# Seven block products for the convolution and gate columns of a fused two-block kernel

## The chip, the cores and the metric

One core of a Trainium2 chip runs the whole program, two residual blocks on a sequence of 1024 tokens of width 1024, in float32 accuracy. The metric is the device time of one execution in microseconds (us), lower is better.

## The reference, cut to what matters

The first block (an HGRN2 mixer and an MLP) is not touched by the change. The second block is

```python
def hybrid_mixer(u, w_in, conv_w, conv_norm_g, ret_norm_g, w_out):
    z = u @ w_in                                    # 1024 x 3584
    cb, cc, ch = jnp.split(z[..., :c0], 3, axis=-1) # 512 columns each
    rq, rk, rv, rg = jnp.split(z[..., c0:], 4, axis=-1)
    y_conv = cb * causal_dwconv3(cc * ch, conv_w)
    y_conv = group_rms_norm(y_conv, conv_norm_g, CONV_GROUPS)   # 8 groups of 64
    q, k = rotary(rq), rotary(rk) * 128 ** -0.5     # 4 heads of 128
    o = chunkwise_retention(q, k, rv)
    y_ret = group_rms_norm(o, ret_norm_g, RET_HEADS) * jax.nn.silu(rg)
    return jnp.concatenate([y_conv, y_ret], axis=-1) @ w_out

h = x + hybrid_mixer(rms_norm(x, norm1_g), ...)
h = h + sq_relu_mlp(rms_norm(h, norm2_g), w_up, w_down)
```

## The kernel before, in words

Activations lie transposed: a tile holds 128 channels (partitions) of all 1024 tokens, in two halves of 512. Every product of float32 is three matmuls in the fp32r type (`mm3`, L200 to L205): each operand is split into a high part (`hi`, `uh`; a cast on ACT) and the rest (`lo`, `ul`; a subtraction on DVE, or on POOL where `self.low` says so), and hi x hi, hi x lo and lo x hi are summed in PSUM. A weight slab is 128 x 1024 (512 KB): it is loaded, split (`split_next`) and used as the stationary operand by `unit`, which makes one output tile for one half of the tokens from eight k tiles, 24 matmuls of 512 columns.

The program is written out once, and the order of the lines is the order on each engine: the engines take their own instructions strictly in turn. Work for the other engines is put between the matmuls by `self.at(delay, fn)`, which has `fn` issued at the end of the tick that comes `delay` ticks later; a `tick` is called after every 12 matmuls of 512 columns. The tables of numbers at the head of the file (`RETENTION_AT` and the like) are such delays. `use` splits a slab now and those up to `look` further on one tick later, and issues the loads; all DMAs are issued by one queue, SP. `slots` is a ring of tiles of 4 KB a partition in SBUF, `bank` and `accb` give PSUM banks, four of each kind.

The MLPs already multiply by seven block products: `expand` makes, for a pair of weight tiles or of operand tiles, the four blocks and the four sums and differences f and g (L832 to L838 for weights, L856 to L862 for operands), splits them, and `group` runs the products in the order P1, P2, P3, P5, P6, P7, P4. `project` multiplies by `w_out`, adds the residual and prepares the MLP's operands.

`mixer2` (L1399 to L1542) goes through these stages. **Values** (about 1192 to 1245 us): the columns of rv, with the token tiles `u` as stationary operand and 256 columns of the weights moving, the first four token chunks k tile by k tile (L1454), the others one after another; the row norms come from PE's `stats` and `turn`, and the residual is rescaled in place (L1444). **Heads** (to 1356): for each of four heads a q and a k slab, rotation on ACT and DVE (L1483 to L1487) and `retention`, whose steps follow by `RETENTION_AT`; its head norm runs in twelve small operations on POOL (L249 to L256) 13 ticks later, and the head's output stays in SBUF as `on[h]`. **Columns** (to 1504): for each of four tiles the slabs cc, ch, cb, with the convolution on ACT and DVE and, per half, `conv_norm`: squares, two matmuls with a matrix of two blocks of ones (L1559), and an iteration for the root on DVE. **Gates** (to 1549): four slabs, Silu and product with `on`. `split_y` (L1496, L1497) splits the convolution's output into the operands of **project** (from 1549), with the low halves on POOL.

Of the kernel before, what the change touches and what calls it, by code (L numbers as in the profile page):

```python
# [11 lines left out]
F32 = mybir.dt.float32  # L12
# [8 lines left out]
P = 128  # L21
# [17 lines left out]
CONV_NORM_AT = (2, 4, 5)  # L39
CONV_SPLIT_AT = (55, 56, 59, 59)  # L40
# [19 lines left out]
HIDDEN_BY = "GVVV"  # L60

# [9 lines left out]
C_CW, C_CG, C_RG, C_ZETA, C_BLK = 320, 332, 336, 340, 344  # L71
C_N = 346
# [25 lines left out]
class Kernel:  # L98
# [483 lines left out]
    def gate(self, ps, half, on, yh, yl, done=None):  # L582
        nc = self.nc
        tk = slice(half * HALF, (half + 1) * HALF)
        z = self.times_rb(ps, half)
# [12 lines left out]
        self.at(GATE_AT[0], product)  # L598
        self.at(GATE_AT[1], low)
# [12 lines left out]
    def run(self):  # L612
# [50 lines left out]
        self.ac = S.get("ac")  # L663
# [45 lines left out]
        self.blocks = sm.tile([P, P], F32R, name="blocks")  # L709

        def set_masks():
            copy = nc.scalar.copy
            for i in range(2):
# [7 lines left out]
            copy(self.blocks.rearrange("p (g f) -> p g f", g=2),  # L721
                 self.col(C_BLK, 2)[:, :, None].to_broadcast([P, 2, 64]))
# [3 lines left out]
        for a in (*self.a_bufs, self.ac[:, :512]):  # L726
            nc.gpsimd.memset(a, 0.0)
# [51 lines left out]
        S.put(*self.a_bufs, self.ac, self.rb)  # L779
# [3 lines left out]
        sp, us, rb = self.project(y, None, C_NMLP, True)  # L783
# [147 lines left out]
    def project(self, y, x, gain, first):  # L931
# [467 lines left out]
    def mixer2(self, x, u, sqs):  # L1399
        nc, S = self.nc, self.slots  # L1400
        self.rb = rb = S.get("rb")
        rx = S.get("rx")
        cos, sin, dx = S.get("cos"), S.get("sin"), S.get("dx")
# [39 lines left out]
        def normed(j):  # L1443
            nc.vector.scalar_tensor_tensor(x[j], x[j], self.col(C_NFIN + j), rx, op0=MUL, op1=MUL)  # L1444
# [55 lines left out]
        for i in range(4):  # L1500
            if i == 0:
                for n in range(4):
                    self.at(CONV_SPLIT_AT[n], lambda n=n: split_y(n))
            cc, yc = S.get("cc"), S.get("yc")
            for part in range(3):
                ws = self.use()
                for half in range(2):
                    tk = slice(half * HALF, (half + 1) * HALF)
                    ps = self.unit(ws[0], u, half)
                    if part == 0:  # L1510
                        nc.vector.tensor_tensor(cc[:, tk], ps, rb[:, tk], op=MUL)
                    elif part == 1:
                        z = self.times_rb(ps, half)
                        nc.vector.tensor_tensor(cc[:, tk], cc[:, tk], z, op=MUL)
                        if half == 1:
                            w = lambda j: self.col(C_CW + 4 * j + i)
                            nc.scalar.activation(yc, cc, AF.Copy, scale=w(2))
                            nc.vector.scalar_tensor_tensor(yc[:, 1:], cc[:, :-1], w(1), yc[:, 1:], op0=MUL, op1=ADD)
                            nc.vector.scalar_tensor_tensor(yc[:, 2:], cc[:, :-2], w(0), yc[:, 2:], op0=MUL, op1=ADD)
                            S.put(cc)  # L1520
                    else:
                        z = self.times_rb(ps, half)
                        nc.vector.tensor_tensor(yc[:, tk], yc[:, tk], z, op=MUL)
                        self.conv_norm(i, yc, half, y)
                self.done(ws)

        self.low = nc.gpsimd
        for j in range(4):
            ws = self.use()
            for half in range(2):  # L1530
                ps = self.unit(ws[0], u, half)
                if half == 0:
                    y[4 + j] = (S.get("yh", F32R), S.get("yl", F32R))
                self.gate(ps, half, lambda j=j: on[j], *y[4 + j],
                          done=(lambda j=j: S.put(on[j])) if half else None)
            self.done(ws)
        self.drain()
        S.put(rb)
        for a in u:
            S.put(*a)  # L1540
        self.low = nc.vector
        return self.project(y, x, C_N2, False)  # L1542

    def conv_norm(self, i, yc, half, y):

        nc, S = self.nc, self.slots
        tk = slice(half * HALF, (half + 1) * HALF)
        A, B = slice(0, HALF), slice(HALF, T)
        n1, n2, n3 = S.get("n1"), S.get("n2", F32R), S.get("n3")
        sq, ms, hi, lo, z, t = n1[:, A], n1[:, B], n2[:, A], n2[:, B], n3[:, A], n3[:, B]  # L1550
        dv = nc.vector
        nc.scalar.activation(sq, yc[:, tk], AF.Square)
        nc.scalar.copy(hi, sq)
        nc.gpsimd.tensor_tensor(lo, sq, hi.bitcast(F32), op=SUB)

        def stat():
            ps = self.bank()
            nc.tensor.matmul(ps, lhsT=self.blocks, rhs=hi, start=True, stop=False)
            nc.tensor.matmul(ps, lhsT=self.blocks, rhs=lo, start=False, stop=True)  # L1559
            dv.tensor_scalar(ms, ps, 1.0 / 64, EPS, op0=MUL, op1=ADD)  # L1560
            dv.tensor_scalar(z.bitcast(I32), ms.bitcast(I32), -0.5, 1597463007.0, op0=MUL, op1=ADD)
# [170 lines left out]
```

## Time and profile before

| | us |
|---|---|
| median of 3 runs | 2269.64 (2268.79 to 2270.84) |
| the profiled execution | 2272.97 |
| its span in the profile | 2270.8 |
| PE busy | 2239.4 (99%) |
| DVE busy | 1768.2 (78%) |
| ACT busy | 880.3 (39%) |
| POOL busy | 405.1 (18%) |

The profile comes from one execution; its own time is 2.2 us more than its span. A row of the timeline gives when an instruction began, how long it lasted, its line, and in brackets how long the engine was idle before it and what ended that. Matmuls overlap each other, so what one costs is read from start to start. In rows of PE the text behind the arrow is the moving operand, then the stationary one.

### The profile page before, as it was taken

What the parts mean: (1) busy time and instruction counts of PE and PEld (TensorE: products, weight loads), DVE (VectorE), ACT (ScalarE), POOL (GpSimd) and SP (SyncE); (2) the same over time, 40 slices, a digit from 0 to 9 for tenths busy, and PEclk for the clock granted to TensorE, in tenths of its full rate; (3) what the DMA queues carried; (4) which work ended last, traced back from release to release, by engine and by line L of the source; (5) the groups of instructions that cost most, each with busy time, mean ns of one, the idle gap of its engine ahead of it and who ended that gap; (6) DMA issues with size and microseconds to landing.
All of it is one profiled execution on the core that took longest, in us unless ns stands there. A gap on an engine that the chain in (4) does not pass through costs nothing.

```text
span 2270.8 us, 32900 instructions
## 1 busy us (share of the span) xinstructions
PE 2239.4 (99%) x13102; PEld 1884.9 (83%) x13102; DVE 1768.2 (78%) x2593; ACT 880.3 (39%) x1346; POOL 405.1 (18%) x381
## 2 busy tenths in 40 slices
PE   8999999999999999999999999999999999999998
PEld 7888797888888888888889888887888888888887
DVE  6857668636888888999996556885698888889996
ACT  6334433434433335434344242224533334533322
POOL 0122112201111111222210011013111111122223
PEclk9999999999999999999999999999999999999999
DMA  4011010123344448444512011112234446744442
GB/s 179 25 36 39 20 38 29 47 76 128 120 169 161 151 168 299 158 148 154 194 43 103 28 40 35 47 38 75 94 137 164 158 153 210 260 152 148 158 158 75
DMA packets 80218, 261.91 MB, mean 115 GB/s; under 512 B 8896, under 2 KB 11456, under 8 KB 80064
## 3 DMA queue, kind: packets, MB, share of 16 engines
q1 hardware_dynamic: 79488, 259.28, 32.8%
q8 instruction: 103, 1.69, 0.3%
q10 hardware_dynamic: 576, 0.52, 0.1%
q14 instruction: 51, 0.42, 0.1%
HBM read 186.37 MB, written 73.40 MB: 114 GB/s over the span
## 4 chain that ended last, share of the span: by engine, by line
PE 86%; DVE 10%; ACT 2%; issue 1%; DMA 1%; SPq 0%; DVEq 0%; ACTq 0%
PE acc L203 20%; PE acc L204 20%; PE acc L205 20%; PE ps L203 7%; PE ps L205 7%; PE ps L204 7%; PE ps L543 1%; PE ps L545 1%; PE ps L523 1%; DVE tmp L579 1%; PE ps L305 1%; DVE tmp L590 1%; DVE ac L389 1%; PE ps L454 0%; DVE lo L174 0%
## 5 line engine op out<-in xcount | busy, mean ns | idle before, releaser
L203 PE MATMUL acc<-hi,hi 128*128 128x512 f32 (+1 forms) x824 | 315.1, 382 | 0.7 <-ACT acc L1226 0.6
L204 PE MATMUL acc<-lo,hi 128*128 128x512 f32 (+1 forms) x824 | 313.9, 381 | 0.7 <-POOL lo L1497 0.7
L205 PE MATMUL acc<-hi,lo 128*128 128x512 f32 (+1 forms) x824 | 313.8, 381 | 0.0
L203 PE MATMUL acc<-uh,hi 128*128 128x512 f32 x768 | 306.6, 399 | 0.0
L204 PE MATMUL acc<-ul,hi 128*128 128x512 f32 x768 | 300.2, 391 | 0.0
L205 PE MATMUL acc<-uh,lo 128*128 128x512 f32 x768 | 300.2, 391 | 0.0
L203 PE MATMUL ps<-hi,hi 128*128 128x512 f32 x712 | 277.2, 389 | 0.0
L205 PE MATMUL ps<-hi,lo 128*128 128x512 f32 x712 | 277.0, 389 | 0.0
L204 PE MATMUL ps<-lo,hi 128*128 128x512 f32 x712 | 277.0, 389 | 0.0
L1169 ACT ACTIVATE hq<-hq 128x512 f32<-128x512 f32 x128 | 81.1, 634 | 336.9 <-DVE hq L1168 269.9
L203 PEld LDWEIGHTS acc<-hi,hi 128*128 128x128 f32 x824 | 154.9, 188 | 31.8 <-ACT acc L1226 1.5
L204 PEld LDWEIGHTS acc<-lo,hi 128*128 128x128 f32 x824 | 154.9, 188 | 31.1 <-POOL lo L1497 1.2
L205 PEld LDWEIGHTS acc<-hi,lo 128*128 128x128 f32 x824 | 154.9, 188 | 29.5
L205 PEld LDWEIGHTS acc<-uh,lo 128*128 128x128 f32 x768 | 144.7, 188 | 31.0
L203 PEld LDWEIGHTS acc<-uh,hi 128*128 128x128 f32 x768 | 144.9, 189 | 30.4 <-ACT v L608 0.2
L204 PEld LDWEIGHTS acc<-ul,hi 128*128 128x128 f32 x768 | 144.9, 189 | 28.9 <-issue 0.5
L204 PEld LDWEIGHTS ps<-lo,hi 128*128 128x128 f32 x712 | 133.6, 188 | 27.9
L205 PEld LDWEIGHTS ps<-hi,lo 128*128 128x128 f32 x712 | 133.6, 188 | 27.7
L203 PEld LDWEIGHTS ps<-hi,hi 128*128 128x128 f32 x712 | 133.6, 188 | 27.7
L180 ACT CAST hi<-h 128x1024 fp32r<-128x1024 f32 x96 | 100.4, 1055 | 134.0 <-DVE lo L181 76.6
L181 DVE TENSOR_TENSOR lo<-h,hi 128x1024 fp32r<-128x1024 f32 x96 | 122.2, 1280 | 6.3 <-ACT hi L180 6.3
L174 DVE TENSOR_TENSOR lo<-w,hi 128x1024 fp32r<-128x1024 f32 x70 | 84.9, 1220 | 49.5 <-ACT hi L173 49.5
(271 smaller groups left out, 4720.5 us busy)
## 6 DMA issues: line engine op xcount, KB each, us to landing
w<-in_w SPq DMA_DIRECT2D x202, 512.0 KB, 4.5
hf<-f SPq DMA_DIRECT2D x28, 512.0 KB, 2.6
hfull<-hq SPq DMA_DIRECT2D x28, 512.0 KB, 3.5
hg<-g SPq DMA_DIRECT2D x28, 512.0 KB, 4.0
h<-hfull SPq DMA_DIRECT2D x28, 512.0 KB, 3.6
h<-hf SPq DMA_DIRECT2D x28, 512.0 KB, 4.4
h<-hg SPq DMA_DIRECT2D x28, 512.0 KB, 3.3
xs<-x SPq DMA_DIRECT2D x16, 512.0 KB, 2.8
```

What stands on the lines that cost most here:

```text
L174: self.low.tensor_tensor(lo, st, hi.bitcast(F32), op=SUB)
L180: self.nc.scalar.copy(hi, src)
L181: self.low.tensor_tensor(lo, src, hi.bitcast(F32), op=SUB)
L203: mm(ps, lhsT=ah, rhs=bh, start=start, stop=False)
L204: mm(ps, lhsT=ah, rhs=bl, start=False, stop=False)
L205: mm(ps, lhsT=al, rhs=bh, start=False, stop=stop)
L305: self.nc.tensor.matmul(ps[:, :n * P], lhsT=self.cs[:, C_ONES:C_ONES + P], rhs=b[:, :n * P], start=True, stop=True)
L389: ve.copy_predicated(av[:, j:], mask[:, v0:v1], pm[:, v0:v1])
L523: nc.tensor.matmul(ps[:, c * P:(c + 1) * P], lhsT=kt[:, t], rhs=v[:, t], start=True, stop=True)
L543: nc.tensor.matmul(o, lhsT=a3[:, i, :], rhs=v[:, t], start=True, stop=(i == 0))
L545: nc.tensor.matmul(o, lhsT=qx[:, t], rhs=s[:, t], start=False, stop=True)
L1169: nc.scalar.activation(t, t, AF.Square)
```

## The change

The 16 slabs of cc, ch, cb and the gates become 8 pairs. For a pair, two output tiles of all 1024 tokens come from seven products instead of eight (each over four pairs of k tiles, 12 matmuls of 512 columns), with blocks of the weights expanded as in the MLP, all sums on POOL (`CONV_BY`), and blocks of the operand: B11, B21, B22 are halves of `u`, the others are sums f and g of the tiles. These sums are made from the scaled residual during the values stage (`block_sums`: two copies of 1024 on ACT, two adds on POOL and two on DVE for each of four pairs of tiles), stored to DRAM, loaded again in the last head and split; f goes over a half of `u`. `four` combines the products into the four quarters of output and hands each to the stage's `out` as PSUM tile and summand. A first and a second pair make cc x ch of two tiles, the third their cb.

The values take 512 columns of weights at a time, four slabs used one after another with `look` 1. `conv_norm` takes two tiles together: eight matmuls with selection matrices bring all sums of squares into one bank, the root is iterated once, and eight matmuls spread it. The residual and the heads' outputs go through DRAM. The matrix `sel` is loaded from a fourth table. In `project` the first tile's second half comes first. The order of the slabs in DRAM follows. A line number of the changed file is 8 higher than before in the helpers (L174 becomes L182, L832 L840, L1497 is now L1640).

```diff
-CONV_NORM_AT = (2, 4, 5)
-CONV_SPLIT_AT = (55, 56, 59, 59)
+BLOCKS_AT = (1, 3, 5, 6)
+T2_AT = (2, 2, 3, 3)
+G_AT = (1, 1, 2, 2)
+CONV_W0_AT = (0, 1, 2, 2, 2, 3)
+CONV_W_AT = (3, 4, 5, 5, 5, 6)
+NORM_AT = (0, 4, 5, 6, 7, 9)
+CONV_SPLIT_AT = (1, 2, 12, 13)
+LATE_SPLIT_AT = (3, 4)
+BLOCKS_BY = "GVGV"
+CONV_BY = "GGGG"
...
 def project(self, y, x, gain, first):
-                if x is None:
-                    xs[j] = S.get("x")
-                    nc.sync.dma_start(xs[j], self.x_dram[j])
-                else:
-                    xs[j] = x[j]
+                xs[j] = S.get("x")
+                nc.sync.dma_start(xs[j], x[j])
                 ws = self.use()
-                for half in range(2):
+                for half in ((1, 0) if n == 0 and not first else (0, 1)):
...
 def mixer2(self, x, u, sqs):
         def normed(j):
...
+            nc.sync.dma_start(xn_dram[j], x[j])
+            S.put(x[j])
...
+        def block_sums(kp):
+            st = {"1": S.get("us"), "2": S.get("us")}
+            for n, j in (("1", kp), ("2", kp + 4)):
+                nc.scalar.activation(st[n], x[j], AF.Copy, scale=self.gg[:, j:j + 1])
+            e = self.expand(st, "B", self.by(BLOCKS_BY))
+            e["sums_f"]()
+            e["sums_g"]()
...
+        for kp in range(4):
+            self.at(BLOCKS_AT[kp], lambda kp=kp: block_sums(kp))
+        self.look = 1
...
+        for n, k in enumerate(order):
+            if n % 2 == 0:
+                ws[k] = self.use()[0]
             for t in range(4):
-                self.col_b(ws, u, t, (k,), banks[t][:, :256], (order[0], order[-1]))
+                values_k(t, k, banks[t])
+            self.tick()
...
+                if h == 3 and dst is k:
+                    w_next = self.prep_w(pairs, CONV_W0_AT, CONV_BY)
+                    for kp in range(4):
+                        self.at(kp, lambda kp=kp: load_blocks(kp, "f"))
+                        self.at(T2_AT[kp], lambda kp=kp: split_t2(kp))
...
+        for kp in range(4):
+            split_t1(kp)
+            self.at(G_AT[kp], lambda kp=kp: load_blocks(kp, "g"))
+            self.at(G_AT[kp] + 2, lambda kp=kp: split_g(kp))
...
+        def pair(out, last=False):
+            i = n_pair[0] = n_pair[0] + 1
+            w = w_next
+            if i < 8:
+                w_next = self.prep_w(pairs + 2 * i, CONV_W_AT, CONV_BY)
+            self.load_to(pairs + 2 * i + 2)
...
+            self.group(w, us, 0, self.four(out), free)
...
+        for i in (0, 2):
+            pair(product(i))
+            pair(product(i + 1))
...
+            pair(gated(i))
+        self.low = p
+        for n in range(4):
+            self.at(CONV_SPLIT_AT[n], lambda n=n: split_y(n))
+        pair(gates(0))
+        self.next_split = self.next_use = pairs + 16
+        self.limit = SECOND_MLP
+        self.at(6, self.split_next)
+        for n in range(2):
+            self.at(LATE_SPLIT_AT[n], lambda n=n: split_y(4 + n))
+        pair(gates(2), True)
...
+        return self.project(y, xn_dram, C_N2, False)
+    def four(self, emit):
...
+        def out(name, ps):
+            if name == "P1":
+                st["p1"] = self.tmp()
+                nc.scalar.copy(st["p1"], ps)
+            elif name in ("P2", "P3", "P5"):
+                st[name] = ps
+                if name == "P2":
+                    emit(0, 0, ps, st["p1"])
+            elif name == "P6":
+                u2 = st["u2"] = self.tmp()
+                v.tensor_tensor(u2, ps, st["p1"], op=ADD)
+                t = self.tmp()
+                v.tensor_tensor(t, st["P5"], u2, op=ADD)
+                emit(0, 1, st["P3"], t)
+            elif name == "P7":
+                u3 = st["u3"] = self.tmp()
+                v.tensor_tensor(u3, ps, st["u2"], op=ADD)
+                emit(1, 1, st["P5"], u3)
+            else:
+                emit(1, 0, ps, st["u3"])
...
 def conv_norm
+        def total(n):
...
+            for c in (A, B):
+                nc.tensor.matmul(st["ps"], lhsT=of(n, 0), rhs=t[:, c], start=(n, c) == (0, A), stop=(n, c) == (3, B))
...
+        def fin(n):
...
+            for c in (A, B):
+                nc.tensor.matmul(ps, lhsT=of(n, 1), rhs=st["s"][:, c], start=c == A, stop=c == B)
+            o = yc[i + r][:, (A, B)[h]]
+            v.scalar_tensor_tensor(o, ps, self.col(C_CG + i + r), o, op0=MUL, op1=MUL)
...
 def retention
+            nc.sync.dma_start(to, on)
```

Three places show how the order moved. The first is DVE at the start of the values stage. `lo` is the low half of a weight slab, `sqs` and `sqg` are sums of squares, `f` and `g` block sums of x, `us` its scaled copy. Before:

```order
L281 SCALAR_TENSOR_TENSOR ul_920_11128<-x_586_8470,gg_6013,uh_919_11127 128x512
L271 TENSOR_TENSOR sqs_897_10777<-sqs_897_10777,tmp887_11156 128x512
L271 TENSOR_TENSOR sqg_898_10778<-sqg_898_10778,tmp888_11158 128x512
L174 TENSOR_TENSOR lo_935_11236<-w_930_11172,hi_934_11235 128x1024
L174 TENSOR_TENSOR lo_937_11240<-w_931_11174,hi_936_11239 128x1024
L246 TENSOR_SCALAR ms895_11325<-acc893_11291 128x8
L247 TENSOR_SCALAR z896_11326<-ms895_11325 128x8
```

and now:

```order
L289 SCALAR_TENSOR_TENSOR ul_919_11126<-x_585_8468,gg_6011,uh_918_11125 128x512
L279 TENSOR_TENSOR sqs_896_10775<-sqs_896_10775,tmp887_11154 128x512
L279 TENSOR_TENSOR sqg_897_10776<-sqg_897_10776,tmp888_11156 128x512
L864 TENSOR_TENSOR f_925_11218<-us_924_11215,f_925_11218 128x512
L869 TENSOR_TENSOR g_926_11221<-us_924_11215,f_925_11218 128x512
L864 TENSOR_TENSOR f_930_11256<-us_929_11253,f_930_11256 128x512
L869 TENSOR_TENSOR g_931_11259<-us_929_11253,f_930_11256 128x512
L182 TENSOR_TENSOR lo_933_11263<-w_921_11186,hi_932_11262 128x1024
```

Two low halves of weights followed the sums of squares directly; now the block sums of two pairs of tiles stand ahead of that of the third slab (`lo_933`), the first two having been split earlier.

The second is POOL between the last head and the first pair. The rows with `t` and `z` are the head norm, `n2` is the low half of a square in the convolution's norm. Before:

```order
L249 TENSOR_TENSOR t1010_12724<-z1009_12723 128x8
L254 TENSOR_TENSOR t1010_12724<-t1010_12724,ms1008_12722 128x8
L255 TENSOR_SCALAR t1010_12724<-t1010_12724 128x8
L256 TENSOR_TENSOR z1009_12723<-t1010_12724,z1009_12723 128x8
L1554 TENSOR_TENSOR n2_1006_12825<-n1_1005_12824,n2_1006_12825 128x512
L1554 TENSOR_TENSOR n2_1009_12859<-n1_1008_12858,n2_1009_12859 128x512
```

and now:

```order
L257 TENSOR_TENSOR t1006_12369<-z1005_12368 128x8
L262 TENSOR_TENSOR t1006_12369<-t1006_12369,ms1004_12367 128x8
L263 TENSOR_SCALAR t1006_12369<-t1006_12369 128x8
L264 TENSOR_TENSOR z1005_12368<-t1006_12369,z1005_12368 128x8
L839 TENSOR_TENSOR f_1000_12384<-w_984_12035 128x512
L840 TENSOR_TENSOR f_1000_12384<-f_1000_12384,w_980_11953 128x512
L844 TENSOR_TENSOR g_1003_12422<-w_980_11953,w_984_12035 128x512
L845 TENSOR_TENSOR g_1003_12422<-w_980_11953,f_1000_12384 128x512
L1576 TENSOR_TENSOR rb2_1015_12478<-rb_920_11161 128x1024
L839 TENSOR_TENSOR f_1038_12612<-w_1021_12486 128x512
```

The weights' four block sums for pair 0 (`f_1000`, `g_1003`) and the square of the row norm (`rb2`) stand behind the head norm, where POOL had next to do with the norm of the first convolution tile.

The third is POOL at the start of the projection. The rows with `yc` and `on` split the operands `y`, the last one the first weight slab. Before (the last `lo` from `w` here is the second slab's, the one above it the first's):

```order
L1497 TENSOR_TENSOR lo_1078_13772<-yc_1012_12865,hi_1077_13771 128x1024
L174 TENSOR_TENSOR lo_1080_13791<-w_1064_13579,hi_1079_13790 128x1024
L1497 TENSOR_TENSOR lo_1084_13828<-yc_1031_13118,hi_1083_13827 128x1024
L1497 TENSOR_TENSOR lo_1086_13832<-yc_1048_13349,hi_1085_13831 128x1024
L174 TENSOR_TENSOR lo_1089_13871<-w_1069_13673,hi_1088_13870 128x1024
```

and now:

```order
L844 TENSOR_TENSOR g_1139_13679<-w_1122_13527,w_1123_13529 128x512
L845 TENSOR_TENSOR g_1139_13679<-w_1122_13527,f_1138_13652 128x512
L1640 TENSOR_TENSOR lo_1153_13808<-on_1125_13549,hi_1152_13807 128x1024
L1640 TENSOR_TENSOR lo_1155_13830<-on_1126_13551,hi_1154_13829 128x1024
L1640 TENSOR_TENSOR lo_1157_13860<-yc_1100_13265,hi_1156_13859 128x1024
L1640 TENSOR_TENSOR lo_1161_13888<-yc_1112_13418,hi_1160_13887 128x1024
L182 TENSOR_TENSOR lo_1163_13892<-w_1145_13721,hi_1162_13891 128x1024
```

The first weight slab (`w_1145`) has moved from among the operands' splits to the end, behind four of them.

## Rows read from the trace of the kernel before

**Rows 1.** The page: busy time, PE in 40 slices, chain by engine

```profile
PE 2239.4 (99%) x13102; PEld 1884.9 (83%) x13102; DVE 1768.2 (78%) x2593; ACT 880.3 (39%) x1346; POOL 405.1 (18%) x381
...
PE   8999999999999999999999999999999999999998
...
PE 86%; DVE 10%; ACT 2%; issue 1%; DMA 1%; SPq 0%; DVEq 0%; ACTq 0%
```

**Rows 2.** By stage: window, length, busy us per engine, PE clock, DMA share, GB/s

```profile
1203.40:1245.50 42.10, 42.10 (x332) 40.09 (x332) 24.22 (x47) 13.36 (x37) 0.00 (x0) 1.00 0.10 32
1358.00:1549.00 191.00, 190.25 (x879) 157.99 (x878) 147.92 (x201) 50.71 (x77) 34.68 (x28) 1.00 0.12 38
```

**Rows 3.** Timeline of PE: start, duration; values, then first columns

```profile
1191.84 0.28 PE L203 MATMUL ps<-hi,uh 128*128 128x256 f32 x1
...
1202.63 0.28 PE L203 MATMUL ps<-hi,uh 128*128 128x256 f32 x1
...
1357.70 0.39 PE L203 MATMUL acc<-uh,hi 128*128 128x512 f32 x1
...
1359.97 0.39 PE L204 MATMUL acc<-ul,hi 128*128 128x512 f32 x1
```

**Rows 4.** Timeline of ACT at the end of the first MLP

```profile
1201.69 0.71 ACT L268 ACTIVATE tmp<-x,cs 128x512 f32<-128x512 f32 x1
1202.31 1.98 ACT L173 CAST hi<-w 128x1024 fp32r<-128x1024 f32 x2
```

**Rows 5.** Timeline of DVE at the end of the first MLP

```profile
1202.29 0.75 DVE L281 SCALAR_TENSOR_TENSOR ul<-x,gg,uh 128x512 fp32r<-128x512 f32 x1
1202.95 0.69 DVE L271 TENSOR_TENSOR sqs<-sqs,tmp 128x512 f32<-128x512 f32 x1
1203.56 0.69 DVE L271 TENSOR_TENSOR sqg<-sqg,tmp 128x512 f32<-128x512 f32 x1
1204.16 2.36 DVE L174 TENSOR_TENSOR lo<-w,hi 128x1024 fp32r<-128x1024 f32 x2
```

**Rows 6.** POOL by line and form: total busy us, mean ns

```profile
L838 POOL TENSOR_TENSOR g<-w,f 128x512 f32<-128x512 f32 x26 | 45.5, 1751 | 55.5 <-DVE f L833 55.5
L832 POOL TENSOR_TENSOR f<-w 128x512 f32<-128x512 f32 x30 | 43.0, 1435 | 272.1 <-DMA w<-in_w 99.5 <-DVE hl L801 86.9 <-PE ps L205 45.9
...
L1497 POOL TENSOR_TENSOR lo<-yc,hi 128x1024 fp32r<-128x1024 f32 x4 | 10.3, 2596 | 7.2 <-ACT hi L1496 7.1
...
L856 POOL TENSOR_TENSOR f<-us 128x512 f32<-128x512 f32 x6 | 7.8, 1298 | 156.6 <-ACT us L947 156.6
```

**Rows 7.** The page's DMA issues: size, us from issue to landing

```profile
xs<-x SPq DMA_DIRECT2D x16, 512.0 KB, 2.8
```

**Rows 8.** Timeline of PE: the first matmul of the column products

```profile
1356.34 0.39 PE L203 MATMUL acc<-uh,hi 128*128 128x512 f32 x1
```

**Rows 9.** Timeline of POOL: last step of the third head's norm

```profile
1356.90 0.20 POOL L256 TENSOR_TENSOR z<-t,z 128x8 f32<-128x8 f32 x1
```

**Rows 10.** Timeline of PE at the start of the output projection

```profile
1545.97 0.39 PE L203 MATMUL acc<-hi,hi 128*128 128x512 f32 x1
1547.10 0.50 PE L204 MATMUL acc<-lo,hi 128*128 128x512 f32 x1 [0.75 <-POOL lo L1497]
...
1549.51 0.39 PE L205 MATMUL acc<-yh,lo 128*128 128x512 f32 x1
1551.11 0.50 PE L203 MATMUL acc<-yh,hi 128*128 128x512 f32 x1 [1.22 <-ACT yh L591]
1551.90 0.50 PE L204 MATMUL acc<-yl,hi 128*128 128x512 f32 x1 [0.28 <-DVE yl L594]
```

**Rows 11.** Timeline of PE at the kernel's start

```profile
5.60 0.58 PE L203 MATMUL acc<-hi,uh 128*128 128x256 f32 x1 [5.60 <-ACT uh L278]
...
10.43 0.41 PE L203 MATMUL acc<-hi,uh 128*128 128x256 f32 x1
...
14.27 0.39 PE L203 MATMUL acc<-hi,uh 128*128 128x256 f32 x1
```

More of the change, by code (lines that the diff above doesn't have):

```diff
@@ L1467, in mixer2 @@
+        for t in range(4, NCH):
+            ps = self.accb()
+            for n, k in enumerate(order):
+                values_k(t, k, ps)
+                if n == 3:
+                    self.tick()
+            self.tick()
+            if t == 4:
+                for i in range(4):
+                    values_out(i, banks[i])
+                self.at(0, lambda: fin(0))
+                self.at(1, lambda: fin(1))
+            values_out(t, ps)
         self.done(ws)
-        self.at(0, lambda: fin(1))
@@ L1469, in mixer2, with load_blocks, split_t2 @@
-        ws = self.use(2)
         self.look = N_LOOK
-        for p in range(4):
-            self.values(self.unit_b(ws, u, p), p, vs[2:], zs)
-        self.done(ws)
+        us = [{} for _ in range(4)]
+        todo = [{} for _ in range(4)]
+        def load_blocks(kp, name):
+            t = todo[kp][name] = S.get(name)
+            nc.sync.dma_start(t, (f_dram if name == "f" else g_dram)[kp])
+        def split_t2(kp):
+            t2 = us[kp]["t2"] = S.get("t2", F32R)
+            self.hilo(t2[:, A], t2[:, B], todo[kp]["f"][:, B])
@@ L1496, in split_y @@
             nc.scalar.copy(hi, t)
-            nc.gpsimd.tensor_tensor(lo, t, hi.bitcast(F32), op=SUB)
+            p.tensor_tensor(lo, t, hi.bitcast(F32), op=SUB)
             S.put(t)
[L1500 to L1536, printed above, removed]
+        def gates(j):
+            def load(r):
+                on[j + r] = S.get("on")
+                nc.sync.dma_start(on[j + r], on_dram[j + r])
+            for r in range(2):
+                self.at(0, lambda r=r: load(r))
+            def out(r, half, ps, other):
+                i = 4 + j + r
+                tk = (A, B)[half]
+                z = self.tmp()
+                v.tensor_tensor(z, ps, other, op=ADD)
+                v.tensor_tensor(z, z, rb[:, tk], op=MUL)
+                if j == 0:
+                    y[i] = on[i - 4]
+                    nc.scalar.activation(z, z, AF.Silu)
+                    self.at(0, lambda: v.tensor_tensor(y[i][:, tk], z, y[i][:, tk], op=MUL))
+                    return
+                if y[i] is None:
+                    y[i] = (S.get("yh", F32R), S.get("yl", F32R))
+                self.gated(z, half, lambda: on[j + r], *y[i],
+                           done=(lambda: S.put(on[j + r])) if half != r else None)
+            return out
@@ L1581, in conv_norm, with squares @@
-        self.at(CONV_NORM_AT[2], fin)
-    def retention(self, h, q, k, v, dx):
+        st = {}
+        blocks = [(r, h) for r in range(2) for h in range(2)]
+        of = lambda n, k: sel[:, k * HALF + n * P:k * HALF + (n + 1) * P]
+        def squares(n):
+            r, h = blocks[n]
+            t = st[n] = S.get("n", F32R)
+            sq = self.tmp()
+            nc.scalar.activation(sq, yc[i + r][:, (A, B)[h]], AF.Square)
+            nc.scalar.copy(t[:, A], sq)
+            p.tensor_tensor(t[:, B], sq, t[:, A].bitcast(F32), op=SUB)
@@ L1584, in retention @@
+        for n in range(4):
+            self.at(NORM_AT[0] + n, lambda n=n: squares(n))
+            self.at(NORM_AT[0] + n + 1, lambda n=n: total(n))
+        for at, fn in zip(NORM_AT[1:5], (stat, step, step, split)):
+            self.at(at, fn)
+        for n in range(4):
+            self.at(NORM_AT[5] + n, lambda n=n: fin(n))
+    def retention(self, h, q, k, v, dx, to):
         nc, S = self.nc, self.slots
```

216 lines of the change are left out of this document (141 added, 75 removed).

## The prediction

> **What bounds the kernel now.** I read the page's first and second parts [rows 1]: TensorE is busy for 2239.4 us, 99% of the span, and no slice falls below eight tenths, so only matmuls taken away, or waits put between them, move the time. The chain that ended last says the same: 86% of it is PE. The profiled execution took 2272.97 us, 3.3 above the median of 2269.64; the sum below is made as a difference and laid on the median. About 0.2%, 4.5 us, is what a measurement can tell from no change.
>
> Then I read the stages. In the windows [rows 2] PE has no idle time in the values stage (42.10 us busy of the 42.10 to 1245.5) and 0.75 us of it in 191 us of convolution and gate columns (1358 to 1549). DVE works 147.92 of those 191 us, ACT 50.71, POOL 34.68. The stage is PE's, but DVE has only 43 us of slack in it, and in-order queues can be late with much less work than that.
>
> **What the change takes from PE.** Start to start, ten 512-wide matmuls take 2.27 us, 0.227 each, and ninety 256-wide ones 10.79 us, 0.120 each [rows 3].
> - Columns: 16 slabs of 48 matmuls are 768; 8 pairs of 7 products of 12 are 672. 96 x 0.227 = -21.8 us.
> - Values: 384 x 0.120 = 46.1 becomes 192 x 0.227 = 43.6: -2.5 us.
> - Conv norm: 16 matmuls become 32 (8 totals and 8 that spread the result, for each two tiles): +3.6 us.
>
> Together **-20.7 us** if PE finds every operand ready. The rest is about where it doesn't. Prices for the counting: ACT 0.6 for 512 columns and 0.99 for 1024 [rows 4]; DVE 0.60 and 1.18 [rows 5], and 0.66 where it does two operations in one; POOL 1.30 at best for a 512 add, 1.44 to 1.75 on average where it does the same block sums in the MLP, 2.60 for 1024 [rows 6]. For the POOL adds I take 1.5, near the two rows of the first sums; 1.3 and 1.75 are the bounds.
>
> **Values: +7.3 us.** The weight slabs now come one after another, so PE wants the third after 48 matmuls, at 1191.84 [rows 3] + 10.9 = 1202.7. ACT comes free of the MLP's squares at 1202.3 [rows 4], but in the new order four copies of x (for the block sums) stand ahead of the cast of that slab: 1202.3 + 5 x 0.99 = 1207.3. Its low half is on DVE behind the sums of two pairs of tiles (first order excerpt), and the second sum waits for POOL's third add: first copy done at 1203.3, three adds to 1207.8, two DVE sums to 1209.0, lo to 1210.2. DVE itself was done with its squares at 1204.2 [rows 5], so it waits for POOL here. In each group of three matmuls the second needs the lo, so one (0.23) runs ahead: 1210.2 - 1202.7 - 0.2 = 7.3 us (6.7 with adds of 1.3, 8 with 1.75). No other work can cover it: PE has nothing else in its order. Fourth slab, norms and turns come out in time. The stores and loads of sums, residual and heads (some 40 more of 512 KB) I cost at nothing: the DMA engines work 0.10 to 0.12 of the time in both stages [rows 2]; if that cover were gone, a late reload of x in the project would cost about one landing, 2.8 us [rows 7].
>
> **Into the first pair: +12 us.** P1 of pair 0 starts where the first column product started, 1356.3 [rows 8], and P3 is due 24 matmuls later, at 1361.8. It needs S3, S4 of the weights. POOL is in the head norm until 1357.1 [rows 9]; then come four adds (second excerpt), to 1363.1, the cast to 1364.1, lo on DVE to 1365.3. Two of the first three matmuls can go ahead (0.45): 3.1 late. From there I counted on in the same way:
> - The second half of the last head's scores wants a PSUM bank that DVE frees by pair 0's first sum, and ten operations of 0.60 (two lo of t2, three of the rotation, four lo of T1, the sum) lie between lo and its end: DVE at 1371.3, PE, ten matmuls of P3 and four of the scores after 1365.3, at 1368.5: 2.8.
> - P7 needs the g blocks of the last two tile pairs; their casts stand on ACT behind the copies of the turned keys, which wait for PE, and then DVE's lo: 2.3.
> - The retention's outputs wait for the state copies behind two sums of pair 0: 1.0; the turn of the head norm for a bank freed behind two lo and the sum u3: 1.8; P3 of pair 1 for POOL's g adds behind the last head norm: 1.0.
>
> Together 12.0; 10.8 at the lowest POOL price, 14 at the highest.
>
> **Later pairs: +6.5 us.** Pairs 2, 3, 5 and 6 come out without a wait. In pair 4 the first conv norm's steps lie on DVE between the sums: from P7 of pair 3 on, 15 operations of 0.62 and two of 1.18 end with the lo that P3 needs at 11.7, PE is there after 48 matmuls at 10.9 (0.4 late); five more DVE steps, a cast and a lo end at 16.0, where PE, at 14.0, wants to spread the result: 1.8 more. In pair 7 the second norm meets the gates, whose Silu on ACT waits for DVE and delays the cast for P3: 1.6 there and 2.6 at the spread. 2.3 + 4.2 = 6.5, between 5 and 8.
>
> **Project start: +4.2 us.** Before, PE waits here some 2.8 us: starts 1.13 apart at 1545.97, 1.60 at 1549.51, 0.79 at 1551.11, where 0.23 is due [rows 10]. Now three lo of 2.60 end POOL's queue, that of the first weight slab last (third excerpt). Counted from the last spread matmul before P4 of pair 7: five DVE operations (3.0), Silu and cast (1.5), then two lo of POOL (5.2) end at 9.7; PE is through P4 at 2.7 and can do two matmuls: 6.6 late, 7.3 with the average POOL price; I take 7.0, less 2.8.
>
> **Sum.** -20.7 + 7.3 + 12.0 + 6.5 + 4.2 = **+9.3 us, 2278.9**. With the waits at their lower counts (6.7, 10.8, 5, 3.8) it is +5.6, at their upper (8, 14, 8, 4.5) +13.8.
>
> **Rivals.**
> 1. *The queues catch up* (ends faster). The waits of the pairs are balances of several engines, and each one that delays PE gives DVE, ACT and POOL time for the next. DVE's 147.92 of 191 us [rows 2] leaves room for it. Then only the two that follow from the order of one queue remain, values and project: -20.7 + 11.5 = -9.2, **2260.4**. Against it: I let each wait shift what follows. It decides at P3 of pair 0: if S3, S4 are split before 1361.8 plus the values' delay, this is the case. With half of the pairs' waits it is 2270.
> 2. *PE is fed throughout*: -20.7, and 2.8 more if the project's wait goes too: **2246 to 2249**. It needs slab 3 of the values split by 1202.7, and ACT is not free before 1202.3 [rows 4]; small.
> 3. *The clock falls in the long gaps* (slower still). After 5.6 us without work the kernel's first 256-wide matmuls come 0.213 apart (18 steps from 10.43 to 14.27) [rows 11], later 0.120 [rows 3], near the ratio of the 1.2 and 2.4 GHz levels; 34 matmuls were slow, 34 x 0.093 = 3.2 us lost. The two longest gaps of the forecast, in the values and at the project, are of 4.6 and some 6 us at a stretch; at 3.2 each the time is **2285.3**. No gap of before in this region is longer than 1.4 us, and the granted clock there is 1.00, so rows say neither yes nor no. The Trainium skill ("TensorE: Matmul & The Clock Gate", section "What's actually happening") has the clock follow how busy the PE was lately, and fall to 1.2 GHz when idle; by that rule this rival is the case. The start of this trace agrees with it, 0.213 against 0.120.
>
> **How the numbers follow.** Forecast, waits of 23 to 36 us with the clock kept: 0.50 (0.06 of it within 4.5 us). Clock: 0.13, slower. Queues catch up, 11 to 23 us of waits: 0.27 (0.17 faster, 0.10 within). Fed throughout: 0.10. So faster 0.27, same 0.16, slower 0.57. The range, 2254 to 2290, takes in the forecast with its bounds, the first rival and the clock; it leaves out the fed PE and clock losses in more than two gaps. The likeliest case alone spans 2272 to 2285.
>
> **What would show it.** Right: some 272 matmuls fewer; a PE gap of about 4.6 us near 1202.9 put down to ACT hi and one of about 2.5 behind it to DVE lo; the third product of pair 0 waiting for DVE lo of g; a gap of 6 to 7 us at the first matmul on y, put down to POOL lo. Wrong: pairs of 19.0 us (84 matmuls) from the first on, or values of 43.6 us with no gap at the third slab. A row spacing of 0.4 us after a gap would show the clock rival.

## The result and the profile after

The changed kernel takes 2306.82 us (2306.39 to 2307.53, 4 runs), beside 2269.84 before on the same chip: ratio 1.0163, 95% interval 1.0146 to 1.0181, 37.0 us slower where 9.3 were forecast. The profiled execution took 2306.47 us. Four lines of its page answer to [rows 1]; the last is the granted clock in 40 slices:

```profile
span 2304.7 us, 32612 instructions
...
PE 2235.9 (97%) x12830; PEld 1865.7 (81%) x12830; DVE 1797.4 (78%) x2588; ACT 912.0 (40%) x1390; POOL 492.7 (21%) x433
...
PE   8999999999999999999989999898999999999998
...
PEclk9999999999999999999999999998999999999999
```

PE has 272 matmuls fewer and is busy for 3.5 us less, but the span is 33.9 us longer, and slices of 8 tenths stand where the second mixer runs. The view of waits, for PE from 1188 to 1585 us, names what its matmuls waited for (total, times, longest); these are its eight longest lines. Before, all waits of this stretch were the three at the project in [rows 10]:

```profile
PE acc L213 <- DVE lo L808: 6.9, 5, 2.2
PE ps L212 <- DVE lo L182: 6.1, 1, 6.1
PE acc L211 <- ACT hi L181: 4.9, 1, 4.9
PE ps L211 <- ACT hi L181: 4.6, 1, 4.6
PE acc L211 <- ACT hi L807: 4.5, 2, 2.4
PE acc L213 <- POOL lo L182: 3.0, 1, 3.0
PE ps L1768 <- ACT n L807: 2.5, 1, 2.5
PE ps L1741 <- POOL n L1734: 2.4, 3, 1.1
```

These are the places that the prediction named: slabs of the values and of the project (L181, L182), the pairs' low halves (L807, L808), the spread and the totals of the norm (L1768, L1741). So the places held, and the sizes did not. Counted start to start, as in the prediction, against 0.227 a matmul (a slow matmul is one that starts some 0.43 us before the next; the 0.1 us by which the first one behind any wait is longer is in the last column too):

| us | forecast | measured | slow matmuls behind the gaps |
|---|---|---|---|
| third value slab | 7.3 | 11.5 | 2.3 |
| last head and pair 0, P3 of pair 1 | 12.0 | 11.6 | 2.6 |
| pairs 3 to 7 | 6.5 | 14.3 | 7.2 |
| project (2.8 before) | 7.0 | 8.5 | 3.2 |
| sum | 32.8 | 45.9 | 15.3 |

-20.7 of work less, -2.8 of waits before, +45.9 + 15.3 make +37.7, and the medians differ by 37.0. Two things are missing in the prediction's sum: 13 us of waits, and 15 us of slow matmuls, which it had left to a rival, the clock. The second line of the table agrees in its sum only; its parts are told behind the experiments. (The spans differ by only 33.9, since the profiled execution of before lay 3.3 above its median; its values began 3.4 us later, of which 1.8 had arisen by 35 us, with the slow matmuls of [rows 11] lasting to 14.27 us instead of 10.6.)

The values stage shows both. PE around the third slab:

```profile
1199.07 0.39 PE L213 MATMUL ps<-hi,ul 128*128 128x512 f32 x1
1204.10 0.79 PE L211 MATMUL ps<-hi,uh 128*128 128x512 f32 x1 [4.64 <-ACT hi L181]
1211.00 0.80 PE L212 MATMUL ps<-lo,uh 128*128 128x512 f32 x1 [6.10 <-DVE lo L182]
1211.60 0.63 PE L213 MATMUL ps<-hi,ul 128*128 128x512 f32 x1
1212.02 0.63 PE L211 MATMUL ps<-hi,uh 128*128 128x512 f32 x1
...
1215.44 0.48 PE L213 MATMUL ps<-hi,ul 128*128 128x512 f32 x1
```

The hi came 4.6 us late, as counted. The low half was due some 2.9 us behind it and took 6.9. DVE and POOL meanwhile:

```profile
1200.11 0.69 DVE L279 TENSOR_TENSOR sqg<-sqg,tmp 128x512 f32<-128x512 f32 x1
1201.96 1.74 DVE L864 TENSOR_TENSOR f<-us,f 128x512 f32<-128x512 f32 x1 [1.16 <-POOL f L863]
1203.73 1.65 DVE L869 TENSOR_TENSOR g<-us,f 128x512 f32<-128x512 f32 x1
1205.31 1.76 DVE L864 TENSOR_TENSOR f<-us,f 128x512 f32<-128x512 f32 x1
1207.10 1.64 DVE L869 TENSOR_TENSOR g<-us,f 128x512 f32<-128x512 f32 x1
1208.66 2.29 DVE L182 TENSOR_TENSOR lo<-w,hi 128x1024 fp32r<-128x1024 f32 x1
```

```profile
1200.13 1.79 POOL L863 TENSOR_TENSOR f<-us 128x512 f32<-128x512 f32 x1 [35.65 <-ACT us L1457]
1201.89 1.26 POOL L868 TENSOR_TENSOR g<-us,us 128x512 f32<-128x512 f32 x1
1203.12 1.72 POOL L863 TENSOR_TENSOR f<-us 128x512 f32<-128x512 f32 x1
1204.80 1.72 POOL L868 TENSOR_TENSOR g<-us,us 128x512 f32<-128x512 f32 x1
1206.47 1.72 POOL L863 TENSOR_TENSOR f<-us 128x512 f32<-128x512 f32 x1
```

DVE's sums of 512 columns last 1.64 to 1.76 us here; the same size a row earlier (`sqg`) and in [rows 5] takes 0.69. Starts on either engine come about 1.7 apart, 0.6 of one and 1.1 to 1.3 of the other: the two engines work in turn. (The DMA engines worked 0.01 of the time from 1199 to 1204, where the first 1.74 stands, so it isn't they; the windows below show this.) The Trainium skill ("SBUF — State Buffer", section "SBUF: two separate sides") has this: a DVE instruction with two inputs in SBUF and a GpSimd one that reads SBUF exclude each other for a whole instruction. These rows agree, 1.7 us for a pair that would take 0.6 and 1.3 side by side. The trace of the kernel before has it too, in the first MLP, where a low half takes 1.73 us beside POOL instead of 1.21, and POOL's sum 2.28 instead of 1.30:

```profile
951.15 1.73 DVE L181 TENSOR_TENSOR lo<-h,hi 128x1024 fp32r<-128x1024 f32 x1
951.76 2.28 POOL L838 TENSOR_TENSOR g<-w,f 128x512 f32<-128x512 f32 x1
```

The POOL averages of [rows 6], 1.44 to 1.75 against 1.30, come from such rows; the prediction took them as a price of POOL's alone.

The clock, by windows of the same stretch (the column behind POOL is the granted clock, the next DMA's share):

```profile
1189.00:1199.00 10.00, 10.00 (x46) 8.29 (x45) 10.00 (x18) 7.48 (x13) 0.00 (x0) 1.00 0.15 52
1199.00:1204.00 5.00, 0.46 (x3) 0.04 (x1) 3.81 (x5) 5.00 (x6) 3.87 (x3) 0.80 0.01 2
1204.00:1211.00 7.00, 0.79 (x1) 0.29 (x1) 6.96 (x5) 6.21 (x7) 5.86 (x4) 0.50 0.84 308
1211.60:1215.00 3.40, 3.40 (x9) 2.65 (x8) 3.40 (x2) 0.00 (x0) 2.77 (x2) 0.50 1.01 399
1215.50:1222.00 6.50, 6.50 (x30) 5.37 (x29) 2.38 (x3) 0.00 (x0) 0.00 (x0) 0.99 0.89 288
```

The clock is 1.00 until PE stops, falls to 0.50 (the 1.2 GHz level) inside the gap, stays there for 3.8 us of work after it, and is 0.99 again behind that. Matmuls come 0.43 us apart in the meantime (1211.60 to 1215.44). The same view of the work behind five later waits, at P3 of pairs 0 and 3, in pairs 4 and 7 and at the project, makes six such places:

```profile
1375.50:1379.40 3.90, 3.90 (x11) 2.98 (x10) 3.87 (x8) 3.90 (x6) 0.00 (x0) 0.50 0.87 343
1454.72:1458.00 3.28, 3.28 (x9) 2.63 (x8) 1.43 (x3) 2.32 (x5) 1.03 (x1) 0.51 0.00 0
1485.50:1488.80 3.30, 3.30 (x9) 2.59 (x8) 3.26 (x4) 1.06 (x2) 0.91 (x1) 0.52 0.00 0
1551.80:1555.20 3.40, 3.40 (x10) 2.62 (x8) 3.21 (x5) 0.63 (x1) 0.00 (x0) 0.50 0.00 0
1579.30:1583.50 4.20, 4.20 (x11) 3.28 (x10) 2.40 (x3) 1.57 (x2) 0.00 (x0) 0.50 0.00 0
```

### The profile page after: what moved, and what is told of

It reads as the page before. It is cut to its first block, busy times and chain, and to the rows that moved or that the text cites. A ratio compares the mean times of both kernels' runs of the same rounds, so it can differ in the third digit from the quotient of the medians.

```text
span 2304.7 us, 32612 instructions
## 1 busy us (share of the span) xinstructions
PE 2235.9 (97%) x12830; PEld 1865.7 (81%) x12830; DVE 1797.4 (78%) x2588; ACT 912.0 (40%) x1390; POOL 492.7 (21%) x433
## 5 line engine op out<-in xcount | busy, mean ns | idle before, releaser
L211 PE MATMUL acc<-hi,hi 128*128 128x512 f32 (+1 forms) x856 | 328.9, 384 | 5.7 <-ACT hi L181 4.9
L213 PE MATMUL acc<-hi,lo 128*128 128x512 f32 (+1 forms) x856 | 327.5, 383 | 3.0 <-POOL lo L182 3.0
L212 PE MATMUL acc<-lo,hi 128*128 128x512 f32 (+1 forms) x856 | 327.4, 382 | 0.0
L211 PE MATMUL acc<-uh,hi 128*128 128x512 f32 x576 | 234.0, 406 | 4.5 <-ACT hi L807 4.5
L213 PE MATMUL acc<-uh,lo 128*128 128x512 f32 x576 | 228.5, 397 | 6.9 <-DVE lo L808 6.9
L212 PE MATMUL acc<-ul,hi 128*128 128x512 f32 x576 | 227.4, 395 | 0.0
L213 PEld LDWEIGHTS acc<-uh,lo 128*128 128x128 f32 x576 | 110.0, 191 | 33.0 <-DVE lo L808 9.3
L211 PEld LDWEIGHTS acc<-uh,hi 128*128 128x128 f32 x576 | 109.9, 191 | 28.3 <-ACT hi L807 5.3
L212 PEld LDWEIGHTS acc<-ul,hi 128*128 128x128 f32 x576 | 110.2, 191 | 21.9 <-issue 0.5
L807 ACT CAST hi<-g 128x1024 fp32r<-128x1024 f32 x80 | 83.6, 1047 | 109.6 <-POOL g L845 92.3
```

Of the source, the lines that this page charges most:

```text
L211: mm(ps, lhsT=ah, rhs=bh, start=start, stop=False)
L212: mm(ps, lhsT=ah, rhs=bl, start=False, stop=False)
L213: mm(ps, lhsT=al, rhs=bh, start=False, stop=stop)
L807: self.nc.scalar.copy(dst_hi, src)
```

## The experiments

The times beside which each stands are those of the kernel before on the same chip, 2269.7 to 2271.1. The changed kernel's interval is 1.0146 to 1.0181. Those of e1, e2, e3, e4, e5, e7 and e10 overlap it, so these totals alone hardly tell a gain or loss of 2 to 7 us, and what such a run shows is read from its rows; those of e6, e8, e9, e11 and e12 lie clear of it.

**Is it POOL that slows DVE?** First in the values (e1):

```diff
-BLOCKS_BY = "GVGV"
+BLOCKS_BY = "VVVV"
```

> All block sums of the values stage on DVE (BLOCKS_BY GVGV becomes VVVV), order unchanged, POOL idle there. In the changed kernel DVE's 512-wide sums there take 1.65 to 1.76 us each while POOL works, 0.68 elsewhere. Theory A, POOL's work beside it slows DVE wherever both operands lie in SBUF: sums come back to about 0.68, DVE does eight before the third slab's low half (4.8 us from 1201), lo ends near 1207; PE's wait falls from 11.5 to about 7 us, time about 2302. Rival B, DVE is slow there for another reason (DMA writing to SBUF, the clock): its sums stay at 1.65, there are twice as many, lo ends near 1216, wait about 17 us, time about 2313.

Ratio 1.0147 (1.0130 to 1.0164): 2305.0, and the waits there are 7.7 us. DVE's rows before the low half:

```profile
1205.95 0.69 DVE L864 TENSOR_TENSOR f<-us,f 128x512 f32<-128x512 f32 x1
...
1207.16 0.68 DVE L869 TENSOR_TENSOR g<-us,f 128x512 f32<-128x512 f32 x1
1207.76 1.22 DVE L182 TENSOR_TENSOR lo<-w,hi 128x1024 fp32r<-128x1024 f32 x1
```

Every sum is back at 0.69, the low half at 1.22, and eight sums take less time than four did beside POOL. The DMA engines work 0.62 of the time there (1202.5 to 1209), and TensorE's granted clock is 0.64, so rival B's causes are there and DVE is not slow. Theory A; the total moved by 3 us, 0.8 less than the wait did.

Then in the pairs, by leaving out work of POOL alone (e9):

```diff
 def product(i): out
-                    p.tensor_tensor(cc[:, tk], cc[:, tk], rb2[:, tk], op=MUL)
 def product(i): conv
-                self.at(1, lambda: p.tensor_tensor(t, t, rb, op=MUL))
```

> Leaves out the products with rb2 and rb that POOL makes in the convolution (8 of 512, 4 of 1024 columns), so the row norm is missing from the convolution; DVE's and ACT's work stays the same in number and order. Theory A, POOL beside it makes DVE late in the pairs too: the some ten operations there that take 1.65 instead of 0.68 come back, waits from pair 1 to the projection fall from 19.7 to about 14, slow matmuls by 2, time about 2300. Rival, DVE is late there by the number and order of its own operations: waits 18 or more, time 2304 to 2307.

Ratio 1.0123 (1.0108 to 1.0138): 2298.0, waits of 15.0 us instead of 19.7, and 3.1 us less of slow matmuls. Busy times of pairs 1 to 7, of the changed kernel and of this one (PE, PEld, DVE, ACT, POOL):

```profile
1408.50:1574.40 165.90, 148.44 (x617) 117.80 (x615) 133.06 (x147) 56.29 (x81) 86.69 (x51) 0.96 0.24 83
```

```profile
1407.00:1565.00 158.00, 144.91 (x617) 116.35 (x615) 125.15 (x147) 56.23 (x81) 66.60 (x39) 0.97 0.26 88
```

With 147 instructions on DVE in both, DVE is busy for 7.9 us less, and P3 of pair 3 no longer waits. So sharing is part of the pairs' waits too. The products cost 4.7 of the 19.7 us, in which the project's first wait of 5.1 is counted; that is not the whole price of sharing, since POOL has other work there, and that the convolution ends sooner without them may be a part of it.

The other way to take POOL's work away is to give it to DVE (e3):

```diff
-CONV_BY = "GGGG"
+CONV_BY = "VVVV"
```

> The weights' block sums of all 8 pairs on DVE instead of POOL (CONV_BY GGGG becomes VVVV): 32 sums of 512 move, 19 us at 0.6. Theory A, sharing with POOL is what made DVE late: DVE's operations in the pairs come back to 0.68 and it ends earlier in spite of the extra work; P3 of pair 0 no longer waits behind the head norm; waits in the pairs fall from about 26 to 15 us, time about 2294. Rival, DVE is the bound by its amount of work: waits grow by some 10 us, time 2316.

Neither: ratio 1.0174 (1.0159 to 1.0189), 2310.3. P3 of pair 0 no longer waits, but P3 of pair 4 waits 4.6 us instead of 2.1, and the waits from pair 1 on stay at 19.1. In pairs 1 to 7 DVE has 23 instructions more than in the changed kernel and is busy for only 5.0 us more, where 23 sums at 0.6 are 14: some 9 us come back where POOL no longer works beside it, and the rest stays in DVE's own queue.

**Is it order alone?** At the third value slab (e2):

```diff
-        for kp in range(4):
-            self.at(BLOCKS_AT[kp], lambda kp=kp: block_sums(kp))
-        self.look = 1
+        self.look = 2
...
                 ws[k] = self.use()[0]
+            if n == 0:
+                for kp in range(4):
+                    self.at(BLOCKS_AT[kp], lambda kp=kp: block_sums(kp))
```

> The third value slab is split one step earlier, ahead of the block sums (look 2, sums planned after the first slab's use); same work otherwise. Theory, the wait is one of order alone: hi done near 1199.9, lo near 1201.1, PE wait at the third slab 1.5 to 2.5 us instead of 11.5, up to 2 us at the fourth; the slow matmuls behind it (3 us) go with the long gap; time about 2295. Rival, the whole stage is short of DVE or POOL time: the wait only moves to the fourth slab (8 us or more there), time 2304 or more.

Ratio 1.0140 (1.0124 to 1.0155): 2302.9, between the two. The third slab waits 2.5 us, the fourth now 3.1, with DVE's sums at 1.7 beside POOL in front of it, and slow matmuls follow both gaps, 3.4 us of them. With the sums on DVE alone as well (e6):

> Both edits of the values stage together: third slab split ahead of the block sums, and the sums on DVE alone. e2 left 2.5 us at the third slab and 3.1 at the fourth, with DVE's sums there at 1.7 us beside POOL. Theory A, the fourth slab's wait comes from the sharing: eight sums of 0.6 end at 1208, lo at 1209, before PE is there at 1210; waits 2.5 us in all, slow matmuls 1.4; time 2306.8 - 10.5 = about 2296. Rival, the copies on ACT hold the fourth slab: 3 us stay there, 2300 or more.

Ratio 1.0116 (1.0101 to 1.0131): 2296.5, as expected by theory A. The waits are 3.3 us in all, 0.8 of them at the fourth slab, and the stage takes 54.3 us instead of 64.5 (53.0 before). Order and sharing make 8.2 of the 11.5 us; the rest is the third slab's low half, for which DVE is not yet out of the squares. The third slab's wait is the same 2.5 us as in e2, but no slow matmuls follow it. The windows behind it in e2 and in e6 differ in the granted clock, 0.50 and 1.00:

```profile
1203.30:1206.60 3.30, 3.30 (x9) 2.55 (x8) 2.52 (x2) 3.30 (x4) 3.30 (x3) 0.50 0.01 2
```

```profile
1203.00:1206.00 3.00, 2.96 (x13) 2.47 (x14) 2.90 (x5) 3.00 (x5) 0.00 (x0) 1.00 0.27 108
```

At the project (e5):

```diff
-        self.at(6, self.split_next)
+        self.at(2, self.split_next)
 def project, second one: order of the k tiles
-                    ps = self.unit(ws[0], y, half)
+                    ps = self.unit(ws[0], y, half, range(KT) if first else (0, 1, 4, 5, 2, 6, 3, 7))
```

> The projection's first weight slab is split four ticks sooner, ahead of the last four operands on POOL, and the second projection sums its k tiles in the order 0,1,4,5,2,6,3,7, the late ones last. Theory, the 8.5 us there are queue order: they fall to about 3.5 us (the fourth convolution tile's low half ends 4 us after the start), the slow matmuls behind them from 3.2 to about 1.5; the changed kernel's 2306.8 goes to about 2300. Rival, ACT and POOL have no room sooner: pair 7 waits as much more, 2305 to 2307.

Ratio 1.0136 (1.0121 to 1.0151): 2301.1, as expected; waits of 3.1 us remain. And at the first pair (e10):

```diff
-                if h == 3 and dst is k:
-                    w_next = self.prep_w(pairs, CONV_W0_AT, CONV_BY)
+                if h == 3 and dst is q:
+                    self.load_to(pairs + 2)
+                    w_next = self.prep_w(pairs, W0_AT, CONV_BY)     # W0_AT = (1, 2, 3, 3, 4, 4)
```

> The first pair's weights are loaded and expanded from the q columns of the last head on, 3 to 4 ticks sooner, so that POOL makes their four sums before the third head's norm instead of behind it. Theory, P3 of pair 0 waits (2.2 and 2.3 us, 2 us of slow matmuls) by that order alone, and the next waits hang on the same chain: 6 to 9 us less, 2298 to 2301. Rival, the head norm, now behind the sums, holds the turn of the heads and the splits of f as much longer: 2304 to 2307.

Ratio 1.0140 (1.0123 to 1.0158): 2303.2, between the two. P3, 4.6 us late before, no longer waits, and slow matmuls are 1.7 us less, but the stage gains only 3.1: the scores behind it now wait 3.3 us instead of 0.8, and keys and states as long as before. The chain was not on P3 alone.

**Is it the clock?** Work that nobody reads, put into the two longest gaps (e4):

```diff
+            if n == 2:
+                spare = self.accb()
+                for _ in range(46):
+                    nc.tensor.matmul(spare, lhsT=u[0][0][:, :P], rhs=u[0][0][:, A], start=True, stop=True)
...
         self.drain()
+        spare = self.bank()
+        for _ in range(34):
+            nc.tensor.matmul(spare, lhsT=sel[:, :P], rhs=sel[:, A], start=True, stop=True)
```

> 46 and 34 matmuls of 512 columns that nobody reads are put on PE into the two longest gaps (before the third value slab, before the projection; 10.4 and 7.7 us), nothing else. The waits were 11.5 and 8.5 us, so the fill costs nothing by itself. Theory, the clock falls in the gaps: the some 20 matmuls at 0.45 us behind these two gaps run at 0.227 again, time 2306.8 - 6 = about 2301. Rival, the slow matmuls are a refill of the pipeline or operands that come late: they stay, time 2306 to 2308.

Ratio 1.0139 (1.0123 to 1.0154): 2302.8, 31.7 above before where the changed kernel is 37.0. PE at the third slab, after the 46 added matmuls:

```profile
1208.74 0.39 PE L211 MATMUL ps<-hi,uh 128*128 128x512 f32 x1
1210.22 0.50 PE L212 MATMUL ps<-lo,uh 128*128 128x512 f32 x1 [1.09 <-DVE lo L182]
1210.56 0.39 PE L213 MATMUL ps<-hi,ul 128*128 128x512 f32 x1
1210.79 0.40 PE L211 MATMUL ps<-hi,uh 128*128 128x512 f32 x1
```

And the window there:

```profile
1208.70:1212.00 3.30, 2.21 (x10) 1.49 (x10) 3.27 (x3) 0.93 (x1) 2.09 (x3) 1.00 1.04 416
```

Behind a wait of 1.1 us the matmuls are at 0.23 at once (0.34 for the first), where they were at 0.43, and the granted clock is 1.00 where it was 0.50. Operands and their order are the same and the DMA engines as busy, so at these two places, the project's rows alike, the slow matmuls were the clock's. For the other four only the granted clock of 0.50 to 0.52 speaks; no experiment was made there. PE did 18 us of useless work and the kernel took 5.3 us less.

**The later pairs.** Steps of the first norm spread out (e7):

```diff
+        norm_at = NORM_AT if i else (0, 4, 7, 10, 13, 15)
```

> The first convolution norm's steps are spread out to ticks 4, 7, 10, 13 and 15 to 18 instead of 4 to 7 and 9 to 12, the second's stay. Theory, its steps on DVE hold the low half that P3 of pair 4 needs and its last step is late for the spread: these waits (2.1, 2.6 and 0.5 us, with 2.5 us of slow matmuls behind) go, time about 2300. Rival, DVE is full over the pairs: the waits come back at P3 of pairs 5 and 6, time 2304 to 2307.

Nearer the rival: ratio 1.0163 (1.0148 to 1.0178), 2308.3. The waits at pair 4 are gone and one of 4.0 us stands in pair 5, where the norm is now spread. The norm left out (e12):

```diff
-        for n in range(4):
-            self.at(NORM_AT[0] + n, lambda n=n: squares(n))
...
+        for r in range(2):
+            y[i + r] = yc[i + r]
```

> Leaves out the convolution's norm (both pairs of tiles: 32 matmuls, 7.3 us of PE, and all its steps on DVE, ACT and POOL). Theory, the waits in pairs 1 to 7 beyond the forecast come from the norm's operations between those of the pairs: of the 14.3 us there (2.6 at pair 3, 5.3 at pair 4, 2.8 at the second totals, 3.6 at P3 of pair 7) at most 3 remain, and of the 7 us of slow matmuls 2; the 8.5 at the projection stay; time 2306.8 - 7.3 - 11 - 5 = about 2283. Rival, the pairs' own sums and splits fill DVE: 9 us or more of waits remain, 2291 or more.

Ratio 1.0072 (1.0056 to 1.0089): 2287.6, between the two. Waits of PE from pair 1 to the project:

```profile
PE acc L211 <- ACT hi L181: 6.7, 1, 6.7
PE acc L213 <- DVE lo L808: 4.3, 3, 3.6
PE acc L211 <- ACT hi L807: 1.4, 1, 1.4
```

The first line is the project's. Of the 14.3 us of pairs 3 to 7 some 6 remain, so the norm's operations make about 8 and the pairs' own sums and splits the rest. The longest that remains, 3.6, is at P3 of pair 3, which waited 1.8 with the norm: POOL now makes the next pair's sums there, and DVE's low half of g takes 2.28 us beside them.

**All together.** The edits of e5, e6 and e7 (e8):

> The edits of e5, e6 and e7 together. If the sites are independent: 6.5 + 10.5 + 6.5 less, about 2283, still 13 us above the kernel before: what is left is the entry into the first pair (11 us of waits, 2.6 of slow matmuls), pair 7 and P3 of pair 3. Rival, a PE that comes sooner finds the next operand late: no more than half of it, 2294 or more.

Ratio 1.0094 (1.0077 to 1.0111): 2290.5, 20.2 above before: 17 less of the 23 expected. In pairs 1 to 7 waits of 13.5 us stay, where the changed kernel has 14.6. Those of e5, e6 and e10, with `CONV_W_AT = (2, 3, 4, 4, 4, 5)` (e11):

> The orders of e5, e6 and e10 together, and the later pairs' weights expanded one tick sooner (CONV_W_AT 2,3,4,4,4,5). Sums: 5.5 + 10.5 + 7 for the three, and 2 to 4 at P3 of pairs 3, 4 and 7 for the last: 2306.8 - 26 = about 2281. Rival, the waits of the pairs go from one product to the next: 2287 or more. In both it stays above the kernel before.

Ratio 1.0103 (1.0088 to 1.0119): 2292.7. The rival: values and project gained as they had alone. Pair 0 gained nothing, its scores now waiting 5.3 us, and pairs 1 to 7 wait 20.0 us, 12.3 of them where the two norms are spread, which cost 3.6 in the changed kernel. No version here beats the kernel before.

## Why the prediction was right in sign and wrong in size

The time, 2306.8, lies outside the range, 2254 to 2290. Right was that the queues would cost more than the seven products save, and, but for pairs 3 and 6, where. Two steps failed: the price of DVE's work while POOL works, and the clock, put at nothing.

- **What PE is spared** held: 272 matmuls fewer.
- **Values, +7.3**: the place, the hi (4.6 counted, 4.64 idle) and the order held (e2, e6). The step that failed is the price, DVE 0.60 and 1.18 [rows 5], while POOL works: 1.7 and 2.3 there. The spread of POOL's prices was put down to POOL alone. Measured 11.5, of which e1 gives 3.8 to the sharing.
- **Into the first pair, +12**: measured 11.6, and this nearness is in part luck. P3 of pair 0 waited 4.6 where 3.1 was counted, the scores 0.8 where 2.8, P3 of pair 1 0.3 where 1.0; keys and P7 together waited 2.7 where 2.3 was counted for P7. The order was as counted, and that one wait shifts the next was right: e10 took away the first, and that of the scores grew to 3.3.
- **Later pairs, +6.5**: measured 14.3. Pairs 3 and 6 were counted as free of waits and have 2.6 and 2.8. In pair 3 the same price failed: DVE's low half of g took 2.32 us beside POOL, PE waited 2.0, and e9, with POOL idle there, has no wait. In pair 6 the norm's totals wait for the squares' low halves on POOL. Pair 4 waited 5.3 where 2.3 was counted, pair 7 3.6 where 4.2. How the 7.8 divide over sharing and count was not settled.
- **Project, 7.0 late**: 8.5, 5.1 of it for the slab's hi and 3.4 for its lo, where only the lo was counted. The product that feeds Silu took 1.83 us beside POOL's low half, and the cast of the slab stands behind that Silu:

```profile
1569.96 1.83 DVE L1656 TENSOR_TENSOR tmp<-tmp,rb 128x512 f32<-128x512 f32 x1
```

- **The clock, 0 in the sum**: 15.3 us of slow matmuls. The third rival had the mechanism and a price for two gaps, 3.2 us each (measured 2.3 and 3.2); the clock fell behind six waits. The prediction gave it little weight because, in the region of the change, rows "say neither yes nor no". The kernel's start, slow after 5.6 us without work, had spoken for it, and so does a place in the first block of the same trace: with waits of 2.31 and 1.08 us the granted clock falls to 0.50, and matmuls of 512 columns come 0.43 apart there.

```profile
375.43 0.66 PE L454 MATMUL ps<-qf,kr 128*32 128x32 f32 x29 [2.31 <-DVE qf L463]
...
376.30:383.00 6.70, 5.62 (x54) 4.41 (x45) 6.19 (x12) 3.15 (x6) 0.00 (x0) 0.50 0.01 2
```

- **The first rival**, that queues catch up, is out: the waits together are 13 us longer than counted, not shorter, and e7, e11 show waits that move on when one is taken away.

## What to carry to other kernels

Where an engine is 99% busy, a saving in its work is worth what the others can deliver in time: count each new operand's place in its producer's queue before the saving. Price a DVE operation with two SBUF inputs at its own time plus POOL's where POOL has work in the same stretch, and read a spread of durations of one form as a sign of it. A gap in PE can cost more than its length: the six places here cost 1.8 to 3.3 us more each in slow matmuls. Not every gap does: behind the same 2.5 us at the third value slab e2 has slow matmuls and e6 has none, and what decides between them no run here shows.

## What was not expected of the hardware

- POOL and DVE do not slow each other in proportion; in the rows here they take turns, and the one that comes second waits out the first (DVE's 512 columns: 1.64 to 1.76 us instead of 0.69 beside 512 of POOL, 2.4 to 2.8 beside 1024). DVE's sums with one operand in PSUM kept 0.69 in the same stretches.
- The clock fell also behind the short waits at P3 of pair 3 (0.5 and 1.8 us idle), where eight matmuls at 0.43 follow; in e6 the same waits (0.4 and 1.8) had none behind them, at a granted clock of 1.00.
- Filling two gaps with matmuls that nobody reads took 5.3 us off (e4).
